# A streaming encoder layer on one core: half the weight differences moved to GpSimd, wider steps at both ends of the state-space loop, gate loads moved to another queue

## The chip, the core and the metric

The kernel runs on one core of a Trainium2 chip. The metric is the device time of one execution in microseconds. TensorE (PE in the rows) multiplies matrices, with a separate row PEld for its weight loads; VectorE (DVE), ScalarE (ACT) and GpSimd (POOL) work element by element; SyncE (SP) mostly issues DMA transfers. Each engine runs its own instructions in order and waits for others by semaphores. PSUM is the memory that PE writes its products to, SBUF the one that tiles live in.

## The reference

One inference step of a one-layer encoder on 2048 new prompt positions and 128 sample positions (8 running streams of 16), with 1024 channels, all in float32:

```
h = RMSNorm(x) * norm_gain
u, g_s, q, k, v, g_a = split(h @ w_in)            # six groups of 512 columns
y_s = S5(u): per channel group a complex diagonal state, h_t = a h_(t-1) + B u_t,
      y = gelu(Re(C h) + D u);  y_s = z_val * sigmoid(z_gate), [z_val, z_gate] = y @ w_glu
y_a = softmax(norm(q) norm(k)^T / 8 + bias(distance)) v      # a band of 9 chunks of 64, 8 heads
y = x + concat[y_s * silu(g_s), y_a * silu(g_a)] @ w_out
```

Outputs are `y`, the newest keys and values, and the final state of the state-space part, for prompt and sample streams.

## The kernel before, in words

The 2176 rows are 17 tiles of 128 (the sample tile first). For accuracy each product of two float32 matrices is three products: every operand is split into a rounded part `hi` and the difference `lo`, and `mm3` (lines 189 to 194) multiplies hi with hi (L192), hi with the weights' lo (L193) and lo with hi (L194).

**The foreground** is a sequence of such products. The input projection runs in three passes over all tiles, with two groups of 512 columns in each: u and k, then v and q, then g_a and g_s. A tile takes 16 calls of `mm3` in a pass, 8 for each group. Then come the GLU (8 calls a tile) and the output projection (16 a tile), 1224 calls in all. After each call `tick` counts a step. Two lists hang on that count: `due` plans the conversions of weight blocks, and `defer` runs a piece of other work some steps later.

**Weights.** A block is 128 rows by 512 columns. `load_w` (L139) loads it by SP's queue into one of five `wraw` buffers, and `conv_w` (L142) makes `whi` on ScalarE and `wlo` on VectorE (L156: raw times gain minus `whi`, in one instruction). The last tile of a pass plans the 16 blocks of the next pass from its step 4 on, 1.25 steps apart, and the background rests until all are issued. Block j of the next pass is numbered from 0 here and is read at step 17 + j of the last tile's count. The load of block j + 5 is issued two steps after the conversion of block j and waits for that buffer.

**Evictions.** Keys and queries are normed: ScalarE squares, VectorE sums (L280), GpSimd takes the power (L281, L282) two steps later, VectorE scales at 8 steps (`zs`, L285), PE transposes at 14 (L295). Keys of the last tiles are also multiplied by a gain on GpSimd (L288) and stored. The gates g_a and g_s are stored to DRAM (L330) from buffers of the tag `plain`.

**The background** is a generator that runs between the steps: the state-space part (`s5`), the decode attention of the 8 sample streams (`decode`), and the band attention. Every foreground step earns credit (650 times a ratio: 0.42 in the state-space loop, 0.75 in decode), and every `yield w` of the background costs w. `SL` is 800 in the state-space part. Its loop has 8 batches of 4 groups, 6 slots a batch. When the u group is done, the loop starts by loading three blocks of u from DRAM (`load_u`, L712), rearranging the first on ScalarE (`perm_u`, L720) and transposing it on PE (`step_a`, L734). In each batch PE makes `v` (L772), VectorE rotates it (L792 to L795), GpSimd makes tables of sine and cosine (L757 to L764). After the loop (L927 to L942) PE transposes the final states (`pf`, `pf2`), VectorE copies them (`of`, `of2`), SP stores them; all three copies use one buffer of the tag `bt`, and all three transposes one PSUM buffer of the tag `ut`. The flag `y`, set at the end, is asked for by the last tile of the third pass, before the first GLU load (L1339).

**The GLU** (`glu`, L1353) loads for each tile the silu gates `gs` (L1376, by SP's queue, into a buffer of the tag `plain`, two of them) when the tile starts, multiplies them into `ms` on GpSimd (L1402) one step into the next tile, and PE transposes `ms` (L1361) after six of the eight steps of that next tile.

Of the kernel before, what the change touches and what calls it, by code (L numbers as in the profile page):

```python
# [7 lines left out]
F32 = mybir.dt.float32  # L8
# [3 lines left out]
OP = mybir.AluOpType  # L12
# [19 lines left out]
def fv(ap):  # L32
    return ap.bitcast(F32)
# [6 lines left out]
class Build:  # L40
# [101 lines left out]
    def conv_w(self):  # L142
        nc = self.nc
        n = self.nconv
        self.nconv += 1
        key, _, k = self.chunks[n]
        raw = self.raws.pop(n)
        hi = self.wp.tile([128, 512], F32R, tag="whi", name="whi", bufs=16)
        lo = self.wp.tile([128, 512], F32R, tag="wlo", name="wlo", bufs=16)
        if k is None:  # L150
            nc.scalar.activation(out=hi, in_=raw, func=AF.Copy)
            nc.vector.tensor_sub(lo, raw, fv(hi))
        else:
            gcol = self.gain[:, k:k + 1]
            nc.scalar.activation(out=hi, in_=raw, func=AF.Copy, scale=gcol)  # L155
            nc.vector.scalar_tensor_tensor(lo, raw, gcol, fv(hi), op0=OP.mult, op1=OP.subtract)  # L156
        self.W[key] = (hi, lo)
        if self.step:
            self.defer(self.T_LW, lambda: self.load_w(n + self.NR))
        elif n + self.NR < 16:  # L160
            self.load_w(n + self.NR)
        else:

            self.defer(40 + 10 * (n + self.NR - 16), lambda: self.load_w(n + self.NR))
# [286 lines left out]
    def s5(self):  # L451
        nc, I, tc = self.nc, self.I, self.tc
# [4 lines left out]
        ps = self.pool(st, "s5ps", side="right", space=PSUM)  # L457
# [91 lines left out]
        g = pp.tile(sh, F32, name="g")  # L549
# [94 lines left out]
        mp = self.pool(st, "s5m", side="right", bufs=2)  # L644
        Tm = []
        for i in range(2):
            t = cp2 = mp.tile([128, GB, 128], F32, name=f"T{i}", bufs=1)
# [3 lines left out]
        CA, VB, VBp, KR, YS = {}, {}, {}, {}, {}  # L651
# [57 lines left out]
        def load_u(b, i):  # L709
            c0, n = BLK[i]  # L710
            u = mp.tile([128, L, GB * CH], F32, tag="U", name="U", bufs=3)
            nc.sync.dma_start(u[0:n], u4[c0:c0 + n, :, b * GB * CH:(b + 1) * GB * CH])  # L712
            U[b, i] = u

        def perm_u(b, i):
            n = BLK[i][1]
            u = U.pop((b, i))
            o = mp.tile([128, GB, L, CH], F32, tag="P", name="P")
            src = u[0:n].rearrange("p j (g h) -> p g j h", g=GB)
            nc.scalar.activation(out=o[0:n], in_=src, func=AF.Copy)  # L720
            P[b, i] = o.rearrange("p g j h -> p g (j h)")
# [131 lines left out]
        SL = self.SL_S5  # L853
# [16 lines left out]
            yield None  # L870
        for n in range(3):
            load_u(0, n)
        yield 2 * SL
        perm_u(0, 0)
        yield SL
        for n in range(3):
            feed(n)
            yield SL
# [48 lines left out]
        pf = ps.tile([32, 128], F32, tag="ut", name="pf")  # L927
        nc.tensor.transpose(pf, FINp, self.ident)
        of = mp.tile([32, 128], F32, tag="bt", name="of", bufs=1)
# [1 line left out]
        nc.sync.dma_start(self.O["rp"], of[:, 0:64])  # L931
        nc.sync.dma_start(self.O["ip"], of[:, 64:128])
        for i in range(2):
            yield 1500
            pf = ps.tile([128, 128], F32, tag="ut", name="pf2")
            nc.tensor.transpose(pf, FINs[:, 4 * i:4 * i + 4].rearrange("p b g -> p (b g)"), self.ident)
            of = mp.tile([128, 128], F32, tag="bt", name="of2", bufs=1)
            nc.vector.tensor_copy(of, pf)
            nc.sync.dma_start(self.O["rs"][128 * i:128 * i + 128], of[:, 0:64])
            nc.sync.dma_start(self.O["is"][128 * i:128 * i + 128], of[:, 64:128])  # L940
# [412 lines left out]
    def glu(self):  # L1353
        nc = self.nc
        W, Z = self.W, {}

        def out(t):
            ms = Z.pop(t)
            pt = self.pst.tile([128, 4, 128], F32, tag="tr", name="tm")
            for k in range(4):  # L1360
                nc.tensor.transpose(pt[:, k], ms[:, 128 * k:128 * k + 128], self.ident)  # L1361
            o = self.ev.tile([128, 8, 128], F32, tag="kt", name="mo", bufs=1)[:, 0:4]
            nc.scalar.activation(out=o.rearrange("p k (c j) -> p k c j", j=L),
                                 in_=pt.rearrange("p k (j c) -> p k c j", j=L), func=AF.Copy, scale=0.5)
            self.defer(2, lambda: nc.sync.dma_start(self.mt_d[t, :, 0:4, :], o))

        for i, t in enumerate(TILES):
            if i == 0:
                self.due(self.step + 16, 10, 8)
            if i == NT - 1:  # L1370
                self.due(self.step + 2, 1.25, 8)
            if i == NT - 2:
                self.out_load(0)
            hi, lo = self.GY.pop(t)
            g = self.ev.tile([128, 512], F32, tag="plain", name="gs")
            nc.sync.dma_start(g, self.gs_d[128 * t:128 * t + 128])  # L1376
            z = {}
            for f in (1, 0):
                z[f] = self.psm.tile([128, 512], F32, tag="mm", name="z")
                for k in range(4):  # L1380
                    self.busy = i == NT - 1
                    self.mm3(z[f], hi[:, k], lo[:, k], W[3, f, k], k == 0, k == 3)
                    self.tick()
                    yield 650
                    if f == 1 and k == 1:
                        if i + 1 < NT:
                            self.glu_conv(TILES[i + 1])
                        else:
                            self.out_conv(0)
                        if i + 2 < NT:  # L1390
                            self.glu_load(TILES[i + 2])
                    if f == 0 and k == 1 and i:
                        out(TILES[i - 1])
                        yield 430
                if f == 1:
                    th = self.ev.tile([128, 512], F32, tag="sq", name="th", bufs=1)
                    nc.scalar.activation(out=th, in_=z[1], func=AF.Tanh, scale=0.5)
            ms = self.ev.tile([128, 1024], F32, tag="vhl", name="ms", bufs=1)[:, 0:512]
            nc.vector.scalar_tensor_tensor(ms, th, 1.0, z[0], op0=OP.add, op1=OP.mult)
            Z[t] = ms  # L1400
            if i + 1 < NT:
                self.defer(1, lambda ms=ms, g=g: nc.gpsimd.tensor_tensor(out=ms, in0=ms, in1=g, op=OP.mult))  # L1402
        nc.vector.tensor_tensor(out=ms, in0=ms, in1=g, op=OP.mult)
        self.defer(4, lambda: out(TILES[-1]))
# [204 lines left out]
```

## Time and profile before

| | us |
|---|---|
| median of 3 runs | 1228.99 (1226.14 to 1230.14) |
| the profiled execution | 1225.45 |
| span of its instructions | 1223.6 |
| mean granted TensorE clock | 0.993 |
| PE, DVE, ACT, POOL busy | 1185.6, 714.5, 610.6, 364.2 |

The order of the work in the trace, in us from the span's start: first pass to about 207, second to about 456, third to 702, GLU to 873, output projection to the end. The state-space loop runs from about 218 to 590, decode from 608 to 670, attention from 715 to 1166. A row's bracket gives how long the engine idled before it and who released it. `PEclk` is the clock that TensorE was granted, as a share of full speed.

### The profile page before, as it was taken

To read this page: it belongs to the slowest core of one execution; us is meant where nothing else is said; L and a number is where in the kernel's file an instruction comes from. 1 tells how busy PE (TensorE), PEld (TensorE's weight loads), DVE (VectorE), ACT (ScalarE), POOL (GpSimd) and SP (SyncE) were. 2 spreads that over 40 slices of the span, in tenths; PEclk is the share of its full clock that TensorE was granted. 3 is DMA by queue.
4 is the path that set the end of the run, shared out by engine and by line. 5 is a ranking of instruction groups with operands and counts; after the bars stand their busy time and mean duration, and the time that the engine had idled before them with its cause. 6 is when DMAs were issued, how large, how long until landed. Compare 5 with 4: busy or idle time off the path is not lost.

```text
span 1223.6 us, 18141 instructions
## 1 busy us (share of the span) xinstructions
PE 1185.6 (97%) x6363; PEld 973.3 (80%) x6363; DVE 714.5 (58%) x1358; ACT 610.6 (50%) x1177; POOL 364.2 (30%) x407
## 2 busy tenths in 40 slices
PE   8999999899999999999899999999999999999998
PEld 6888888678788887787667878788788788888887
DVE  5476627489888888963234336665655555555511
ACT  6435436465555666553243446555655455555510
POOL 2433562267757647530000011111211111111120
PEclk9999999999999999999999999999999999999999
DMA  7765456757466778445796598998578687778143
GB/s 251 241 193 167 150 169 202 219 140 168 119 170 159 160 223 196 103 111 94 212 349 232 160 270 247 265 263 228 196 227 237 185 221 231 211 210 256 57 132 117
DMA packets 250018, 236.78 MB, mean 194 GB/s; under 512 B 111256, under 2 KB 184736, under 8 KB 248904
## 3 DMA queue, kind: packets, MB, share of 16 engines
q1 hardware_dynamic: 248408, 232.16, 66.4%
q0 software_dynamic: 1376, 3.47, 1.0%
q8 instruction: 50, 0.82, 0.3%
q14 instruction: 40, 0.33, 0.1%
q10 hardware_dynamic: 144, 0.00, 0.0%
HBM read 169.48 MB, written 68.06 MB: 194 GB/s over the span
## 4 chain that ended last, share of the span: by engine, by line
PE 78%; DMA 9%; DVE 5%; ACT 4%; SPq 3%; issue 2%; POOL 0%; DVEq 0%; ACTq 0%; POOLq 0%
PE z L192 18%; PE z L194 18%; PE z L193 18%; PE o L1221 5%; PE pt L1203 5%; PE s L1173 5%; DMA wraw<-in_w_in_dram 3%; PE pt L295 1%; PE v L772 1%; PE y L841 1%; PE y L840 1%; DMA mt<-mt_d 1%; PE o L1062 1%; DMA vc<-in_vc_dram 1%; DVE hlo L232 1%
## 5 line engine op out<-in xcount | busy, mean ns | idle before, releaser
L192 PE MATMUL z<-whi,hhi 128*128 128x512 f32 x816 | 342.0, 419 | 0.8 <-ACT whi L155 0.7
L193 PE MATMUL z<-wlo,hhi 128*128 128x512 f32 x816 | 321.1, 394 | 2.4 <-DVE wlo L156 2.4
L194 PE MATMUL z<-whi,hlo 128*128 128x512 f32 x816 | 320.9, 393 | 0.0
L192 PEld LDWEIGHTS z<-whi,hhi 128*128 128x128 f32 x816 | 154.5, 189 | 36.3 <-issue 3.3
L193 PEld LDWEIGHTS z<-wlo,hhi 128*128 128x128 f32 x816 | 154.5, 189 | 35.6 <-DVE wlo L156 6.1
L194 PEld LDWEIGHTS z<-whi,hlo 128*128 128x128 f32 x816 | 154.1, 189 | 33.7
L1210 ACT ACTIVATE pth<-pt 128x640 fp32r<-128x640 f32 (+4 forms) x128 | 81.7, 638 | 133.8 <-PE pt L1203 95.5
L1211 DVE TENSOR_TENSOR ptl<-pt,pth 128x640 fp32r<-128x640 f32 (+4 forms) x128 | 94.5, 739 | 54.2 <-ACT pth L1210 53.2
L1192 ACT ACTIVATE sn<-sn,mn 128x640 f32<-128x640 f32 (+4 forms) x128 | 96.9, 757 | 36.0 <-DVE mn L1183 34.1
L192 PE MATMUL z<-whi,mh 128*128 128x512 f32 x272 | 114.4, 420 | 0.0
L194 PE MATMUL z<-whi,ml 128*128 128x512 f32 x272 | 107.5, 395 | 0.0
L193 PE MATMUL z<-wlo,mh 128*128 128x512 f32 x272 | 107.2, 394 | 0.0
L1183 DVE CUSTOM_DVE_ANT_0 sn<-s,bias 128x640 f32<-128x640 f32 (+4 forms) x128 | 93.2, 728 | 7.2 <-PE s L1173 7.0
L1203 PE MATMUL pt<-ident,sn 128*128 128x128 f32 x560 | 83.1, 274 | 9.7 <-DVE ptl L1211 6.4
L1402 POOL TENSOR_TENSOR ms<-ms,gs 128x512 f32<-128x512 f32 x16 | 20.7, 1291 | 230.9 <-DMA gs<-gs_d 119.5
L1173 PE MATMUL s<-ks,q 128*128 128x320 f32 (+1 forms) x448 | 88.1, 313 | 0.2 <-DVE mn L1183 0.2
L1203 PEld LDWEIGHTS pt<-ident,sn 128*128 128x128 f32 x560 | 64.7, 140 | 29.5 <-ACT sn L1192 12.8
L1173 PEld LDWEIGHTS s<-ks,q 128*128 128x128 f32 x448 | 75.5, 189 | 13.1 <-DVE mn L1183 3.0
L1417 POOL TENSOR_TENSOR ml<-mt,mh 128x1024 fp32r<-128x1024 f32 x17 | 40.6, 2390 | 126.8 <-ACT mh L1416 95.1
L232 DVE TENSOR_TENSOR hlo<-xraw,hhi 128x1024 fp32r<-128x1024 f32 x49 | 60.8, 1241 | 20.7 <-ACT hhi L229 18.8
L1238 POOL TENSOR_TENSOR ga<-ga,sum 128x512 f32<-128x512 f32 x16 | 16.7, 1044 | 171.6 <-DVE sum L1236 123.6
L281 POOL TENSOR_SCALAR s<-s 128x8 f32<-128x8 f32 x34 | 15.1, 445 | 176.5 <-DVE s L280 176.1
(261 smaller groups left out, 2111.7 us busy)
## 6 DMA issues: line engine op xcount, KB each, us to landing
xraw<-in_xT_dram SPq DMA_DIRECT2D x49, 512.0 KB
q<-qt_d SPq DMA_DIRECT2D x64, 256.0 KB
ks<-kt_d SPq DMA_DIRECT2D x28, 512.0 KB
vhl<-vp_d SPq DMA_DIRECT2D x28, 512.0 KB
wraw<-in_w_in_dram SPq DMA_DIRECT2D x48, 256.0 KB
bias<-tl_d SPq DMA_DIRECT2D x32, 320.0 KB
mt<-mt_d SPq DMA_DIRECT2D x17, 512.0 KB
x<-in_x_dram SPq DMA_DIRECT2D x34, 256.0 KB
```

Source lines behind the costliest of these rows:

```text
L192: mm(z, a, whi, start=first, stop=False)
L193: mm(z, a, wlo, start=False, stop=False)
L194: mm(z, b, whi, start=False, stop=last)
L232: nc.vector.tensor_sub(lo, raw, fv(hi))
L1173: nc.tensor.matmul(ps_s[:, bank, 0:wp], Q[n, x2][:, s, 128 * a:128 * a + 128], KS[n][:, s, c0:c0 + wp], start=(x2 == 0), stop=(x2 == 1))
L1183: nc.vector.tensor_tensor_reduce(out=o, in0=i0, in1=i1, scale=1.0, scalar=3e38, op0=OP.add, op1=OP.min, accum_out=mn)
L1192: nc.scalar.activation(out=sn[:, 0:w], in_=sn[:, 0:w], func=AF.Exp, scale=-1.0, bias=mn, accum_out=SUM[n][:, a, s:s + 1])
L1203: nc.tensor.transpose(t[:, k], pr[:, 128 * k:128 * k + 128], self.ident)
L1210: nc.scalar.activation(out=h, in_=t[:, 0:w], func=AF.Copy)
L1211: post.append(lambda: nc.vector.tensor_tensor(out=l, in0=t[:, 0:w], in1=fv(h), op=OP.subtract))
L1221: nc.tensor.matmul(o[:, a0:a1], VB[n][:, j, s, :], t[:, 3 * a0 + j + a0:4 * (a1 - 1) + j + 1:4], start=(y == 0 and j == 4), stop=(y == 1 a ...
L1417: self.defer(2, lambda: self.nc.gpsimd.tensor_tensor(out=lo, in0=m, in1=fv(hi), op=OP.subtract))
```

## The change

At input pass changes (the first index of the block's key is 1 or 2) the `lo` of odd blocks is made on GpSimd in two instructions, the first of which overwrites `raw`. At the start of the state-space loop 5 SL instead of 2 SL lie between the loads of u and the first `perm_u`, and 2 SL instead of one behind it. At its end 2500 instead of 1500 of credit lie ahead of each of the last two transposes, these use PSUM buffers of the tags `y` and `v` (two each), and the first of the two copies uses a buffer of the tag `VB` (two of them). The load of the GLU's gates is issued by GpSimd's queue.

```diff
@@ conv_w @@
-            nc.vector.scalar_tensor_tensor(lo, raw, gcol, fv(hi), op0=OP.mult, op1=OP.subtract)
+            if key[0] and n % 2:
+
+                nc.gpsimd.tensor_scalar(raw, raw, gcol, None, op0=OP.mult)
+                nc.gpsimd.tensor_tensor(out=lo, in0=raw, in1=fv(hi), op=OP.subtract)
+            else:
+                nc.vector.scalar_tensor_tensor(lo, raw, gcol, fv(hi), op0=OP.mult, op1=OP.subtract)
@@ s5, start of the loop @@
         for n in range(3):
             load_u(0, n)
+        yield 5 * SL
+        perm_u(0, 0)
         yield 2 * SL
-        perm_u(0, 0)
-        yield SL
         for n in range(3):
             feed(n)
             yield SL
@@ s5, end @@
         for i in range(2):
-            yield 1500
-            pf = ps.tile([128, 128], F32, tag="ut", name="pf2")
+            yield 2500
+            pf = ps.tile([128, 128], F32, tag=("y", "v")[i], name="pf2", bufs=2)
             nc.tensor.transpose(pf, FINs[:, 4 * i:4 * i + 4].rearrange("p b g -> p (b g)"), self.ident)
-            of = mp.tile([128, 128], F32, tag="bt", name="of2", bufs=1)
+            of = mp.tile([128, 128], F32, tag=("VB", "bt")[i], name="of2", bufs=(2, 1)[i])
@@ glu @@
             g = self.ev.tile([128, 512], F32, tag="plain", name="gs")
-            nc.sync.dma_start(g, self.gs_d[128 * t:128 * t + 128])
+            nc.gpsimd.dma_start(g, self.gs_d[128 * t:128 * t + 128])
```

## Rows read from the trace of the kernel before

**Rows 1.** The page's part 1: busy us, share of the span, instructions.
```profile
PE 1185.6 (97%) x6363; PEld 973.3 (80%) x6363; DVE 714.5 (58%) x1358; ACT 610.6 (50%) x1177; POOL 364.2 (30%) x407
```

**Rows 2.** Timeline of PE at four places: start, duration, instruction, [idle before <- releaser].
```profile
216.62 0.50 PE L193 MATMUL z<-wlo,hhi 128*128 128x512 f32 x1 [0.46 <-DVE wlo L156]
...
219.27 0.63 PE L295 MATMUL pt<-ident,zs 128*128 128x128 f32 x4 [1.93 <-DVE zs L285]
...
224.57 1.11 PE L734 MATMUL ut<-ident,P 128*128 128x128 f32 x4 [3.29 <-ACT P L720]
...
465.71 0.72 PE L772 MATMUL v<-UT,VB 128*128 128x272 f32 x2 [2.32 <-DVE t L792]
...
585.78 0.33 PE L936 MATMUL pf<-ident,FINs 128*128 128x128 f32 x1 [2.32 <-DVE of L938]
...
714.80 0.65 PE L1361 MATMUL tm<-ident,ms 128*128 128x128 f32 x4 [2.50 <-POOL ms L1402]
```

**Rows 3.** Windows: length; busy (count) of PE, PEld, DVE, ACT, POOL; clock, DMA, GB/s.
```profile
224.38:227.79 3.41, 3.22 (x10) 2.74 (x11) 1.54 (x4) 3.38 (x7) 0.09 (x1) 0.50 1.05 349
...
715.90:719.31 3.41, 3.16 (x9) 1.95 (x8) 1.24 (x2) 2.12 (x4) 0.00 (x0) 0.50 1.05 353
978.73:982.14 3.41, 3.41 (x12) 2.81 (x11) 1.99 (x4) 1.68 (x4) 0.66 (x1) 0.50 1.06 187
```

**Rows 4.** Single lines over the whole span: count, duration in ns minimum/median/maximum.
```profile
L156 DVE SCALAR_TENSOR_TENSOR wlo<-wraw,gain,whi x48: 741/751/1876, 4.9 to 463.5; 128x512 fp32r<-128x512 f32 x48
...
L1402 POOL TENSOR_TENSOR ms<-ms,gs x16: 1256/1296/1305, 713.5 to 868.0; 128x512 f32<-128x512 f32 x16
...
L281 POOL TENSOR_SCALAR s<-s x34: 192/197/1399, 33.1 to 460.0; 128x8 f32<-128x8 f32 x34
...
L282 POOL TENSOR_TENSOR s<-s,nhalf x34: 1636/1678/2732, 34.2 to 460.7; 128x8 f32<-128x8 f32 x34
...
L762 POOL TENSOR_TENSOR sin<-sb,cb x32: 609/798/1602, 147.3 to 526.8; 128x256 f32<-128x256 f32 x32
```

**Rows 5.** Timelines of ACT, DVE and POOL at the first pass change.
```profile
197.86 2.56 ACT L155 ACTIVATE whi<-wraw,gain 128x512 fp32r<-128x512 f32 x4
...
202.58 2.54 DVE L156 SCALAR_TENSOR_TENSOR wlo<-wraw,gain,whi 128x512 fp32r<-128x512 f32 x2
202.62 1.29 POOL L288 TENSOR_TENSOR plain<-zs,kgrow 128x512 f32<-128x512 f32 x1 [3.40 <-ACT whi L155]
...
223.88 0.63 ACT L720 ACTIVATE P<-U 128x512 f32<-128x512 f32 x1 [6.14 <-DMA U<-u_d]
```

**Rows 6.** Timelines of POOL and PE at the second pass change.
```profile
444.50 2.05 POOL L282 TENSOR_TENSOR s<-s,nhalf 128x8 f32<-128x8 f32 x1
...
450.21 0.60 PE L295 MATMUL pt<-ident,zs 128*128 128x128 f32 x4
457.48 0.62 PE L772 MATMUL v<-UT,VB 128*128 128x272 f32 x2
...
467.14 1.05 PE L295 MATMUL pt<-ident,zs 128*128 128x128 f32 x4
```

**Rows 7.** DVE's timeline at the loop's end; line L1339 over the whole span.
```profile
585.43 0.29 DVE L938 COPY of<-pf 128x128 f32<-128x128 f32 x1 [8.86 <-DMA out_dram<-of]
...
L1339 SPq DMA_DIRECT2D y<-y_d x17: 370/431/599, 689.7 to 841.3; - x17
```

**Rows 8.** Chain and SP's timeline at the GLU's start; DMA issues (KB each, us to landing).
```profile
704.69 8.65 DMA gs<-gs_d
...
714.77 0.34 SPq L1376 DMA_DIRECT2D gs<-gs_d  x1
...
tl_d<-rl_d POOLq DMA_DIRECT2D x8, 383.5 KB, 5.4
...
rl_d<-rl POOLq DMA_DIRECT2D x1, 24.0 KB, 2.8
```

## The prediction

> **What bounds the kernel now.** I read the page's engine totals first: TensorE (PE) is busy 1185.6 of 1223.6 us and no other engine over 60% [rows 1], so the time is that of PE's stream, and only time in which PE waits or runs slowly can be won: 38.0 us of waits, plus what the clock takes. The timeline of PE then says where the long waits lie. The reader is to see three places in [rows 2] where one wait is 2.3 us or more beside a cause that the diff touches (585.8, 714.8 and 465.7), and a fourth, around 216 to 225, where three waits follow each other (0.46, 1.93 and 3.29). Third, the windows on the granted clock: after each of these four places, and once more at 978.73, there are 3.41 us at a granted clock of 0.50, the lower of the two levels (1.2 of 2.4 GHz) [rows 3] (three of the five stand there); PE had idled 2.32, 2.50 or 3.29 us just before, while after the wait of 1.93 us it went on at the upper level. 3.41 us at half speed lose 1.71 us each.
>
> So the four places cost: first pass change 0.46 + 1.93 + 3.29 + 1.71 = 7.4; second pass change 2.32 + 1.71 = 4.0; end of the state-space loop 2.32 + 1.71 = 4.0; start of the GLU 2.50 + 1.71 = 4.2. Together 19.6 us. The sum is made against the profiled execution, 1225.45 us with a span of 1223.6; the median of the runs shown is 3.54 us above it, and I carry the difference over to that median.
>
> A scheduling step is three products. From the turn's transposes at 450.21 (after step 14 of a tile, 0.45 us in all) to the first background product at 457.48 (after step 24) there are ten: (7.27 - 0.45) / 10 = 0.68 us of PE each [rows 6]. In the state-space phase it gives the background 0.42 x 650 = 273 of credit.
>
> **Wider step at the loop's start.** At 224.57 PE waits for `ut`, which waits for `perm_u` on ScalarE, which sat 6.14 us until the first U block landed [rows 5]. The transposes are issued 3 SL = 2400 of credit after the loads, 8.8 steps; in the change 7 SL = 5600, 20.5 steps, so 11.7 steps or 8.0 us of products more lie between. That is over the 6.14 us waited, so this wait (3.29) goes. The cost of the later start is put at nothing: the loop's end gates the foreground only at the first GLU load, issued at 689.7 [rows 7], while the loop's last transposes stand at 585.8 [rows 2]; 19 steps (below) are 13 us of over 100.
>
> **Half the differences on GpSimd (POOL).** Eight of sixteen at each change leave VectorE, 8 x 0.751 = 6.0 us per change [rows 4], and become two POOL instructions each. The second is like L1402 (same shape, two inputs): 1.296. The first, one input over 512 columns, is not in the trace; the bounds are 0.197 (8 columns, L281) and 1.296 (two inputs, L1402); I take half of the latter, 0.65, as it reads half as much. What VectorE does meanwhile stretches POOL: L762 takes 0.609 alone and 0.798 at the median. I add 0.25 to each of the two (0.19 for 256 columns, rounded up for 512): 2.44 us per block. Bounds: 0.197 + 1.296 = 1.5, and 2 x 1.296 + 1.0 (both stretched by L762's maximum less its minimum, 0.99, in half of them) = 3.6.
>
> These blocks stand in POOL's queue with the power of the key or query norm (L281 and L282, 0.197 + 1.678, up to 2.7 beside VectorE [rows 4]; I take 2.2 for both), which is issued between blocks 11 and 13. Queued behind it are block 13, block 15 and the sine tables; VectorE's `zs` waits for the power, PE for `wlo`. PE reads block j at step 17 + j of the last tile's count; the turn's transposes (L295) follow step 30, so the product just ahead of them reads block 13.
>
> First change: PE reads `wlo` 13 at 216.62, already 0.46 late [rows 2]. POOL can start block 1 when the first ScalarE conversions are done, at about 199.2 [rows 5]; six blocks are 14.6, the key product in between 1.29, so block 11 ends near 215.1, the power (2.2) 217.3, block 13 219.7, block 15 222.2. Before, block 15 was read some 1.4 us after the transposes of 219.27, at 220.7. PE thus reaches it 1.5 later (1.7 with the clock), the 1.93 lies inside the new wait, the 3.29 and its clock fall go, and a wait of some 3.5 us brings a clock fall of its own, already paid in the 1.7 but for 0.3: 1.7 + 0.3 - 3.3 - 1.7 = -3.0. From the bounds: at 1.5 per block nothing waits but `zs` behind the power, -6.5; at 3.6 block 15 ends at 231.5, +10.8 - 5.0 = +5.8.
>
> Second change: POOL is free of the last power at 446.55 [rows 6]; block 11 ends at 461.2, the power 463.4, block 13 465.8, block 15 468.3. The wait of 2.32 for VectorE's `t` goes, since the last difference and `zs` no longer stand ahead of it so long; PE comes to block 13 about 462.5 (457.48, five steps of 0.68, and some 1.6 us of background products between) and waits to 465.8. Before, it read it about 466.5 (the step ahead of the turn at 467.14) and block 15 about 469.5 (two steps at the lower clock later). So the place breaks even: 0. Bounds: -4.0 at 1.5 per block; at 3.6, block 15 at 477.6, +8.
>
> The raw buffers of odd blocks come free about 1.7 us later, and SP's in-order queue holds the next loads with them; costed at nothing because the load of the last block hangs on blocks 5 and 10, of which one is odd (inside the bounds otherwise).
>
> VectorE and POOL share something: L156 takes 0.741 at best and 1.876 at most [rows 4]; the two of it at 202.58 take 2.54 where POOL's key product of 1.29 runs beside them [rows 5]. The Trainium skill, "SBUF — State Buffer", section "Who interferes with whom", says that a VectorE instruction with two SBUF inputs and a GpSimd instruction that reads SBUF shut each other out for a whole instruction. By that rule the two engines' times add, 1.94 + 0.75 for a pair of blocks and what else VectorE takes between, towards the 3.2 per block of the late-POOL rival below, 1229. The trace agrees for that one pair of rows; L762's median, 0.798 against a maximum of 1.602, says that most do not wait that long.
>
> **Wider step and other buffers at the loop's end.** At 585.78 PE waits 2.32 for VectorE's copy `of2`, which had waited 8.86 for the store of the one `bt` buffer [rows 2, 7]. The first `of2` now takes a VB buffer that nothing uses, the second `bt` 5000 / 273 = 18.3 steps = 12.5 us after `of`, more than the 8.86 us that the release took. PE's transposes get PSUM buffers of their own. -4.0. If SP's queue ran 3.6 us later the wait would come back in part: bounds -4.0 to 0.
>
> **Gates by POOL's queue.** PE waits at 714.80 for `ms`, POOL's product, which waited for the gate load of 704.69, 8.65 us on its way [rows 2, 8]. On POOL's queue it is issued no later. The landing of a load of 256 KB there isn't shown; bounds are 2.8 us (24 KB, the shortest of that queue) and 8.65 (as now), the nearest is 5.4 us for 383.5 KB [rows 8]: landed at 710.1, product done at 711.4, PE comes at 712.1. -4.2; if not, 0. New order on POOL: the next tile's load is issued ahead of the product. It waits for a buffer: in tile 1 that is held by the last silu store; behind it waits the first product, and PE for that. POOL, busy 30% [rows 1], has room for the 17 issues. SP loses 17 issues and a hold: at 714.77 it waited for that product with a bias load behind it [rows 8]. Attention's first loads, 19 steps later now, no longer crowd these.
>
> The Trainium skill, "DMA: Bandwidth & Descriptors", section "Issuing engines are not separate DMA queues", says that DMAs from all engines interleave on the same sixteen, and that another issuer saves its issue time only. By that the load lands as late as now and this part gives 0; no run here shows 256 KB on both queues.
>
> **The rest.** 4 SL = 11.7 steps and 2000 / 273 = 7.3 more shift the loop, the decode stage and attention against the tiles. PE's other waits are 38.0 - 12.8 = 25 us over 1224, about 2 per 100 us; some 490 us are re-drawn, 10 us of waits. I take +1 (bounds -3 and +4).
>
> **Sum:** -3.0 + 0 - 4.0 - 4.2 + 1 = -10.2, so 1215.3 for the profiled execution and **1219** for the median. Its own range: 1214 to 1225.
>
> **Rivals.**
> *POOL is cheap* (1.5 to 1.7 per block): -6.5 - 4.0 - 4.0 - 4.2 + 1 = -17.7, 1211. For it: POOL is idle 70%. Against: the power in its queue, and L762's stretch.
> *The gates land no earlier* (the transfers share engines, or the first load is held for the store): -6.0, 1223. For it: the chain shows this load as slow, not its issue as late. Against: the transfers crowding it move away.
> *POOL becomes the late one at both changes*, slower: the price is eight times what a block takes over 2.44, in each change. At 3.2 per block +2.6 and +5, with -8.2 + 1: no change; from there on slower, at 3.6 5.8 + 8 - 8.2 + 1 = +6.6, 1236. For it: L156's 1.876; the rule of the Trainium skill on the shared port ("SBUF — State Buffer") leads here. Against: VectorE has eight such instructions fewer to bring at each change.
> *Re-phasing eats it*: the loop's VectorE-heavy part falls just behind the second change: +5 instead of +1, and 0 from the start of the GLU: -2, 1227.
>
> **Chances.** Forecast 0.50 (faster 0.46, same 0.04); cheap POOL 0.17 (faster); late gates 0.13 (0.09, 0.04); late POOL 0.15 (same 0.06, slower 0.09); re-phasing 0.05 (0.02, 0.02, 0.01). A measurement of this kernel tells 0.3%, 3.7 us, from no change: faster 0.74, same 0.16, slower 0.10. Range 1210 to 1230: the cheap case inside its lower end, late POOL up to no change inside its upper end.
>
> **What would show it.** Right: no PE wait for `ut`, `pf` or the first `tm`; three stretches at 0.50 instead of five; waits for `wlo` of some 3 us just ahead of the turn's transposes at both changes, on POOL. Wrong: POOL blocks of 1.7 us with no wait for `wlo` (too little forecast), or of over 3 us; the gate load landing after 8 us; waits for `t` or `zs` behind the second change.

## The result: slower by 0.9%

The changed kernel takes 1238.56 us (1237.42 to 1239.15), the kernel before, run beside it, 1227.57: ratio 1.0091, interval 1.0075 to 1.0106. 1219 with a range of 1210 to 1230 was forecast.

### The profile page after: what moved, and what is told of

It is laid out like the page before. It is cut to its first block, busy times and chain, and to the rows that moved or that the text cites. A ratio compares the mean times of both kernels' runs of the same rounds, so it can differ in the third digit from the quotient of the medians.

```text
span 1236.2 us, 18182 instructions
## 1 busy us (share of the span) xinstructions
PE 1189.3 (96%) x6363; PEld 974.1 (79%) x6363; DVE 712.5 (58%) x1342; ACT 611.9 (50%) x1177; POOL 426.8 (35%) x456
## 4 chain that ended last, share of the span: by engine, by line
PE 85%; DMA 4%; ACT 3%; DVE 3%; POOL 2%; issue 2%; SPq 0%; POOLq 0%; DVEq 0%; ACTq 0%
PE z L197 21%; PE z L199 20%; PE z L198 20%; PE o L1226 5%; PE pt L1208 5%; PE s L1178 5%; DMA wraw<-in_w_in_dram 2%; POOL wraw L158 1%; PE pt L300 1%; PE y L845 1%; PE y L846 1%; PE v L777 1%; PE o L1067 1%; DMA mt_d<-mo 1%; PE ut L739 1%
## 5 line engine op out<-in xcount | busy, mean ns | idle before, releaser
L197 PE MATMUL z<-whi,hhi 128*128 128x512 f32 x816 | 342.2, 419 | 0.2
L198 PE MATMUL z<-wlo,hhi 128*128 128x512 f32 x816 | 322.4, 395 | 19.4 <-POOL wlo L159 17.6
L199 PE MATMUL z<-whi,hlo 128*128 128x512 f32 x816 | 321.2, 394 | 0.0
L197 PEld LDWEIGHTS z<-whi,hhi 128*128 128x128 f32 x816 | 154.2, 189 | 35.5 <-issue 3.3
L199 PEld LDWEIGHTS z<-whi,hlo 128*128 128x128 f32 x816 | 154.2, 189 | 33.6 <-DVE hlo L237 0.3
L197 PE MATMUL z<-whi,mh 128*128 128x512 f32 x272 | 115.3, 424 | 1.9 <-ACT mh L1421 1.9
L199 PE MATMUL z<-whi,ml 128*128 128x512 f32 x272 | 107.9, 397 | 1.9 <-POOL ml L1422 1.9
L286 POOL TENSOR_SCALAR s<-s 128x8 f32<-128x8 f32 x34 | 11.3, 332 | 157.2 <-DVE s L285 156.7
L1236 DVE TENSOR_TENSOR ot<-o,tmp 64x512 f32<-64x512 f32 x32 | 22.0, 689 | 74.7 <-ACT tmp L1234 74.7
```

What stands on the lines that cost most here:

```text
L197: mm(z, a, whi, start=first, stop=False)
L198: mm(z, a, wlo, start=False, stop=False)
L199: mm(z, b, whi, start=False, stop=last)
```

## The profile after

The changed kernel's lines stand five below those of before from L162 on: the differences are L158 and L159 on POOL and L161 on VectorE, `mm3` is L197 to L199. PE's timeline at the two pass changes, the answer to the first rows of [rows 2]:

```profile
214.00 0.51 PE L198 MATMUL z<-wlo,hhi 128*128 128x512 f32 x1 [1.67 <-POOL wlo L159]
...
216.89 0.50 PE L198 MATMUL z<-wlo,hhi 128*128 128x512 f32 x1 [1.24 <-POOL wlo L159]
...
220.78 0.50 PE L198 MATMUL z<-wlo,hhi 128*128 128x512 f32 x1 [2.21 <-POOL wlo L159]
...
226.25 0.79 PE L198 MATMUL z<-wlo,hhi 128*128 128x512 f32 x1 [2.98 <-POOL wlo L159]
...
470.91 0.50 PE L198 MATMUL z<-wlo,hhi 128*128 128x512 f32 x1 [1.27 <-POOL wlo L159]
...
477.33 0.80 PE L198 MATMUL z<-wlo,hhi 128*128 128x512 f32 x1 [4.32 <-POOL wlo L159]
```

None of the waits of [rows 2] is left at its place. In their place PE waits for odd blocks made by POOL, ten times, 17.6 us together. The windows of the changed kernel, the two pass changes, the stretch from the loop's end through decode, and the end of attention (columns as in [rows 3]):

```profile
205.00:240.00 35.00, 26.81 (x105) 20.17 (x104) 12.73 (x17) 14.32 (x22) 26.52 (x19) 0.85 0.73 223
440.00:490.00 50.00, 40.54 (x172) 31.32 (x171) 32.02 (x47) 27.72 (x51) 39.81 (x31) 0.97 0.70 202
560.00:700.00 140.00, 140.00 (x1050) 108.44 (x1049) 53.44 (x138) 54.75 (x100) 0.96 (x1) 1.00 0.68 211
1160.00:1200.00 40.00, 34.25 (x161) 27.29 (x160) 10.63 (x19) 8.09 (x13) 5.79 (x3) 0.96 0.29 96
```

The last two of the same windows in the kernel before:

```profile
560.00:700.00 140.00, 134.58 (x1019) 103.57 (x1018) 42.32 (x109) 48.77 (x83) 0.96 (x1) 0.99 0.70 218
1160.00:1200.00 40.00, 38.83 (x179) 31.85 (x180) 8.13 (x14) 6.07 (x8) 9.50 (x5) 1.00 0.42 135
```

From the loop's end through decode PE never stops now (140.00 of 140.00, before 134.58); at attention's end it works 34.25 of 40 us, before 38.83. The lower clock at the first change lasts far longer than the 3.41 us of [rows 3]:

```profile
221.30:231.45 10.15, 7.17 (x19) 5.21 (x19) 2.65 (x4) 1.89 (x3) 8.87 (x6) 0.50 0.68 205
```

To add up such places I take, for each microsecond of the profile, what PE idled plus its busy time x (1 - granted clock), and call it lost:

| place (us) | before | changed | difference | forecast |
|---|---|---|---|---|
| first pass change, 205 to 240 | 7.2 | 11.8 | +4.6 | -3.0 |
| second pass change, 440 to 490 | 4.3 | 11.1 | +6.7 | 0 |
| loop's end and decode, 490 to 700 | 7.8 | 0.0 | -7.8 | -4.0 |
| start of the GLU, 700 to 750 | 4.5 | 6.0 | +1.4 | -4.2 |
| end of attention, 1160 to 1200 | 1.2 | 7.4 | +6.2 | in the +1 |
| all else | 20.6 | 20.4 | -0.2 | in the +1 |
| sum | 45.6 | 56.7 | +11.0 | -10.2 |

The profiled spans differ by 12.6; 1.6 us of it are not in this table. A place repeats to about 2 us, little more than a clock fall, from one execution to the next: four kernels below that change nothing ahead of 560 us lose 6.8 to 9.1 and 2.6 to 4.8 at the two pass changes, where the kernel before loses 7.2 and 4.3.

At the start of the GLU the wait for the first gated product is gone, but attention's first score now waits for VectorE, and PE goes on at the lower clock (0.50 from 737.37 to 741.00):

```profile
737.37 0.79 PE L1178 MATMUL s<-ks,q 128*128 128x256 f32 x2 [2.85 <-DVE mn L1188]
```

POOL's timeline shows the cause at the first change:

```profile
212.68 1.26 POOL L159 TENSOR_TENSOR wlo<-wraw,whi 128x512 fp32r<-128x512 f32 x1
213.92 1.57 POOL L158 TENSOR_SCALAR wraw<-wraw,gain 128x512 f32<-128x512 f32 x1
215.58 1.26 POOL L159 TENSOR_TENSOR wlo<-wraw,whi 128x512 fp32r<-128x512 f32 x1
216.82 1.57 POOL L158 TENSOR_SCALAR wraw<-wraw,gain 128x512 f32<-128x512 f32 x1
218.47 2.26 POOL L159 TENSOR_TENSOR wlo<-wraw,whi 128x512 fp32r<-128x512 f32 x1
220.81 0.20 POOL L286 TENSOR_SCALAR s<-s 128x8 f32<-128x8 f32 x1
221.09 1.68 POOL L287 TENSOR_TENSOR s<-s,nhalf 128x8 f32<-128x8 f32 x1
222.76 2.08 POOL L158 TENSOR_SCALAR wraw<-wraw,gain 128x512 f32<-128x512 f32 x1
224.93 1.26 POOL L159 TENSOR_TENSOR wlo<-wraw,whi 128x512 fp32r<-128x512 f32 x1
```

In these rows a block is 2.9 to 3.9 us, not the 2.44 forecast, and PE's waits above end where the subtractions end. Behind the sixth stands the power (L286, L287), behind that block 13, for which PE waits longest (2.98). The two lines over the whole span (columns as in [rows 4]):

```profile
L158 POOL TENSOR_SCALAR wraw<-wraw,gain x16: 1566/2004/2650, 199.2 to 477.3; 128x512 f32<-128x512 f32 x16
...
L159 POOL TENSOR_TENSOR wlo<-wraw,whi x16: 1262/1285/2256, 201.3 to 480.0; 128x512 fp32r<-128x512 f32 x16
```

Together 53.5 us in 16 blocks, 3.34 each. The instruction that I took at 0.65 takes 1.57 at best and 2.00 at the median.

## Experiments

Medians in us of 6 or 12 executions; the kernel before was run beside each group of four, and the ratio is to that.

| kernel | median | before | ratio, interval |
|---|---|---|---|
| no_pool | 1223.2 | 1226.4 | 0.9966, 0.9944 to 0.9987 |
| pool_only | 1239.6 | 1226.4 | 1.0097, 1.0073 to 1.0121 |
| steps_only | 1221.6 | 1226.4 | 0.9956, 0.9934 to 0.9979 |
| gates_only | 1229.9 | 1226.4 | 1.0020, 0.9999 to 1.0042 |
| start_only | 1233.9 | 1226.2 | 1.0064, 1.0045 to 1.0084 |
| end_only | 1218.3 | 1226.2 | 0.9931, 0.9907 to 0.9955 |
| pool_quarter | 1230.7 | 1226.2 | 1.0036, 1.0022 to 1.0049 |
| pool_bcast | 1230.3 | 1226.2 | 1.0041, 1.0026 to 1.0057 |
| pool_to11 | 1230.9 | 1225.9 | 1.0044, 1.0022 to 1.0066 |
| end_start4 | 1220.6 | 1225.9 | 0.9950, 0.9928 to 0.9971 |
| end_start3 | 1227.4 | 1225.9 | 1.0008, 0.9987 to 1.0029 |
| all_margin | 1227.9 | 1225.9 | 1.0020, 1.0004 to 1.0036 |
| end_margin | 1214.8 | 1225.9 | 0.9911, 0.9889 to 0.9933 |
| end_pool3 | 1223.4 | 1225.9 | 0.9978, 0.9963 to 0.9994 |
| end_gates | 1220.2 | 1225.9 | 0.9957, 0.9936 to 0.9977 |

### Each part alone

**no_pool**: the change without its first hunk.

```diff
-            if key[0] and n % 2:
...
-            else:
-                nc.vector.scalar_tensor_tensor(lo, raw, gcol, fv(hi), op0=OP.mult, op1=OP.subtract)
+            nc.vector.scalar_tensor_tensor(lo, raw, gcol, fv(hi), op0=OP.mult, op1=OP.subtract)
```

> All of the change but the differences on GpSimd. Price theory (GpSimd's 3.3 us per odd block paces both pass changes, where TensorE loses 11.8 and 11.1 us by waits and clock): the first change falls back to the two early waits of before, 2.4 us, the second to about 4.3, so 16.2 us less than the changed kernel: 1222 us, and no wait for wlo over 0.5. Re-phasing theory (the later background, not GpSimd's price, is what made it slower): it stays above the kernel before, 1230 us or more, with the waits near the end of attention (5.8 us of idle from 1160 to 1200) still there.

**pool_only**: the kernel before with that hunk alone.

```diff
+            if key[0] and n % 2:
+                nc.gpsimd.tensor_scalar(raw, raw, gcol, None, op0=OP.mult)
+                nc.gpsimd.tensor_tensor(out=lo, in0=raw, in1=fv(hi), op=OP.subtract)
...
```

> The kernel before with the differences of odd blocks at the pass changes on GpSimd and nothing else. Price theory: +4.6 at the first change (the wait for the first U block lies inside the new waits) and +6.7 at the second: 1239 us, as slow as the whole change, with the waits of 2.3 at the loop's end and 2.5 at the first GLU product still there. Re-phasing theory: half of that at most, 1233 or less.

In their totals both came out as the price theory has it: without POOL's blocks 1223.2, with nothing but them 1239.6. The GpSimd part costs 12 to 15 us (by ratios and by medians), as much as the whole loss or more. The end of attention still loses 5.5 in no_pool, so that part of the re-phasing theory held as well.

By places the theory fits less well. It put no_pool at 2.4 and 4.3 at the pass changes, and no_pool loses 3.9 and 8.1; pool_only loses 14.7 and 9.2 there, and 4.1 more than the kernel before from 490 to 700. So in the changed kernel POOL's blocks add 7.9 at the first change and 3.0 at the second. The other 3.8 at the second (8.1 against 4.3) come with the step at the loop's start: steps_only loses 8.0 there, start_only 6.8. In these kernels SP issues transfers for the loop (U and T, nine of them from 436.84 to 443.36 in no_pool) shortly ahead of the weight loads, and ScalarE waits longer for block 5. Its timelines, in the kernel before and in no_pool:

```profile
450.55 2.80 ACT L155 ACTIVATE whi<-wraw,gain 128x512 fp32r<-128x512 f32 x4 [2.88 <-DMA wraw<-in_w_in_dram]
```

```profile
451.64 2.82 ACT L155 ACTIVATE whi<-wraw,gain 128x512 fp32r<-128x512 f32 x4 [6.93 <-DMA wraw<-in_w_in_dram]
```

The same wait is 6.51 in steps_only, 5.17 in start_only and 5.35 in the changed kernel, where POOL too starts block 5 after a wait of 2.54 for its load (457.85). That this order in SP's queue makes up the 3.8 is read from the traces and wasn't tested.

**steps_only** and **gates_only**: the kernel before with the two hunks of the state-space loop, and with the last hunk.

```diff
-        yield 2 * SL
+        yield 5 * SL
         perm_u(0, 0)
-        yield SL
+        yield 2 * SL
...
-            yield 1500
+            yield 2500
```

> The kernel before with both wider steps of the state-space part and nothing else. By the ledger of the changed kernel: -5.0 (wait for ut and its clock fall) -4.0 (loop's end) and, if the later attention costs what it shows there, +1.4 at its first scores and +6.2 at its end: 1226 us. If the waits at attention's start and end come from the GpSimd part or the gates instead: 1218.5.

```diff
-            nc.sync.dma_start(g, self.gs_d[128 * t:128 * t + 128])
+            nc.gpsimd.dma_start(g, self.gs_d[128 * t:128 * t + 128])
```

> The kernel before with the gate loads on GpSimd's queue and nothing else. If the queue brings them early enough: the wait of 2.5 us for the first gated product goes with its clock fall, 1223.4 us. If the transfers share what they shared before: within 1 us of the kernel before, 1227.6, with that wait still over 1.5 us.

steps_only lies between its two numbers; in its trace PE no longer waits for the first gated product, though SP still loads the gates: the first load goes out at 694.38, ahead of attention's first `q` loads at 705.52. So the steps, not the queue, took that wait away. gates_only made it longer. POOL's timeline there, and PE's product behind it:

```profile
698.40 0.59 POOL L1376 DMA_DIRECT2D gs<-gs_d  x1 [103.70 <-DMA gs_d<-plain]
716.97 0.55 POOL L1376 DMA_DIRECT2D gs<-gs_d  x1 [17.98 <-DMA gs_d<-plain]
717.54 1.27 POOL L1402 TENSOR_TENSOR ms<-ms,gs 128x512 f32<-128x512 f32 x1
```

```profile
718.87 1.12 PE L1361 MATMUL tm<-ident,ms 128*128 128x128 f32 x4 [5.55 <-POOL ms L1402]
```

The first load goes out 6.3 us earlier than in [rows 8], but the second then holds POOL's queue for 17.98 us, until its buffer is stored, and the first product, queued behind it, cannot start before 717.54. PE waits 5.55 where it waited 2.50.

**start_only** and **end_only** part the two steps.

> The kernel before with the wider step at the loop's start alone. Both theories: the wait for ut and its clock fall go (-5). Price theory of the pair of steps: the 12 steps of shift are what makes the wait for zs at the second change 3.3 us instead of the 2.3 for t (+3.7 with the clock), and the loop's end keeps its 4.0: 1225. If the shift at the second change comes from the other step: 1221.

> The kernel before with the wider step, the PSUM and the SBUF buffers at the loop's end alone. The wait of 2.3 for of2 and its clock fall go (-4.0) and everything ahead of 560 us stays as it was, so 1222.4; if 7 steps of delay are enough to move the attention loads off the first gate load, that wait goes too: 1218. If the end of attention then waits as it does with both steps (+2.2): 1220 to 1225.

The edits are the first and the second half of the hunks above. end_only gains more than the wait and its clock fall: what is lost from 560 to 700 falls from 7.1 to 1.7, and the wait for the first gated product goes too. start_only is slower than the kernel before, and outside both of its numbers. The wait for `ut` goes, as forecast, but PE's timeline shows what comes instead, the first of these with 2.8 us more lost to the clock:

```profile
597.41 0.48 PE L936 MATMUL pf<-ident,FINs 128*128 128x128 f32 x1 [5.08 <-DVE of L938]
...
729.28 0.80 PE L1173 MATMUL s<-ks,q 128*128 128x256 f32 x2 [3.65 <-DVE mn L1183]
```

The second is attention's first score, and 1160 to 1200 loses 6.7. Of the 7.7 us by which the profiled span is longer, the end of attention makes +5.5, the second change +2.5, the start of the GLU +1.9 and the first change -2.7; from 490 to 700 the kernel loses 7.8, as before. The wait of 5.08 is for the one `bt` buffer. SP issues the store that frees it 9.4 us after the copy (594.39 after 585.03), behind eight stores of y begun at 584.78; before, it was 5.4 us (581.98 after 576.57).

### What a block on POOL costs

**ts_imm**, **pool_bcast**: the first of the two instructions in two other forms; ts_imm leaves the gain out of these differences.

```diff
-                nc.gpsimd.tensor_scalar(raw, raw, gcol, None, op0=OP.mult)
+                nc.gpsimd.tensor_scalar(raw, raw, 1.0, None, op0=OP.mult)
```

> The whole change with the constant 1 in place of the gain column in GpSimd's first instruction (the gain is left out of these differences). If reading the column is what makes it 1.57 us alone and 2.0 beside VectorE: 1.3 or less, and no longer where VectorE is busy at its start. If it is the one-input form itself: 1.5 to 1.6 again, still 2.0 where it starts during a VectorE instruction.

```diff
-                nc.gpsimd.tensor_scalar(raw, raw, gcol, None, op0=OP.mult)
+                nc.gpsimd.tensor_tensor(out=raw, in0=raw, in1=gcol.to_broadcast([128, 512]), op=OP.mult)
```

> The whole change, but the product with the gain is made by an instruction with two tensor inputs (the gain column repeated along the row) instead of one with a column scalar. If that form takes the 1.27 us of the subtraction, a block costs 2.6 instead of 3.3, and each change is shorter by up to 8 x 0.75 = 6 us: 1227 to 1231. If two instructions with two inputs shut VectorE out, or are shut out, for as long: a block still costs 3.2 or more, 1236 or more.

The lines over the span, of ts_imm with one row of POOL's timeline behind it, then of pool_bcast:

```profile
L158 POOL TENSOR_SCALAR wraw<-wraw x16: 1487/1499/2038, 199.4 to 474.2; 128x512 f32<-128x512 f32 x16
...
210.17 1.94 POOL L158 TENSOR_SCALAR wraw<-wraw 128x512 f32<-128x512 f32 x1
```

```profile
L158 POOL TENSOR_TENSOR wraw<-wraw,gain x16: 1030/1318/1526, 200.2 to 471.8; 128x512 f32<-128x512 f32 x16
...
L159 POOL TENSOR_TENSOR wlo<-wraw,whi x16: 1261/1600/1753, 201.8 to 473.3; 128x512 fp32r<-128x512 f32 x16
```

With a constant the one-input form still takes 1.49 at best, so it is the form that is slow; the column adds 0.08. The stretch beside VectorE stays: the seven of the 16 that started 0.06 us or more into a two-input VectorE instruction took 1.93 to 2.04 (the row above started at 210.17, VectorE's difference ran from 209.50 to 210.76), the other nine 1.49 or 1.50. The median falls from 2.00 to 1.50 because fewer started so. That is ts_imm's second theory. With two inputs the product takes 1.03 alone, but then the subtraction's median rises from 1.29 to 1.60. ts_imm, in one run, took 1232.35; pool_bcast is 6 to 8 us below the whole change (by ratios and by medians), as its first theory had the time; a block takes 2.78 on average, between the 2.6 and the 3.2 of the two theories.

**pool_quarter**, **pool_to11**: fewer blocks on POOL, in the whole change.

```diff
-            if key[0] and n % 2:
+            if key[0] and n % 4 == 1:
```

> The whole change with only blocks 1, 5, 9 and 13 on GpSimd, the other twelve on VectorE. Queue theory (GpSimd is late only because 8 blocks of 3.3 us do not fit ahead of PE's reads): 4 blocks take 13.4 us, the first three are done ahead of PE's first read of them, so no wait for wlo over 1 us: 1223, as without the GpSimd part. Linear theory (each block moved costs its share): half of the loss stays, 1231.

```diff
-            if key[0] and n % 2:
+            if key[0] and n % 2 and n % 16 < 12:
```

> The whole change, but blocks 13 and 15, the two that stand behind the power of the key or query norm in GpSimd's queue, stay on VectorE. Place theory (what stands behind the power costs most): the waits of 2.98 and 4.32 us and the lower clock behind them go, those for the blocks up to 11 stay (5.1 and 4.7 us): 10 us less than the whole change, 1228. Share theory (six of eight blocks cost six eighths of the 16 us): 1234.5.

pool_quarter's time is what the linear theory says, but its rows are those of a queue: PE's long waits are both for block 13, the one behind the power:

```profile
224.11 0.79 PE L198 MATMUL z<-wlo,hhi 128*128 128x512 f32 x1 [4.67 <-POOL wlo L159]
...
472.84 0.80 PE L198 MATMUL z<-wlo,hhi 128*128 128x512 f32 x1 [5.18 <-POOL wlo L159]
```

pool_to11 takes that block away, and at the first change 6.8 us are lost instead of 11.8, as the place theory has it; the time lies between the two theories. At the second change nothing is won (12.6 against 11.1): six of VectorE's instructions for the state-space loop, 471.33 to 477.99, are late next, and PE waits for what follows them (DVE's timeline, then PE's):

```profile
471.33 1.17 DVE L664 TENSOR_TENSOR CA<-PB,ArS 128x576 f32<-128x576 f32 x1
...
477.00 0.99 DVE L675 TENSOR_TENSOR VBp<-VBp,btmp 128x512 f32<-128x512 f32 x1
```

```profile
478.38 1.27 PE L777 MATMUL v<-UT,VB 128*128 128x272 f32 x2 [3.84 <-DVE t L797]
```

**end_pool3**: the loop's end with only blocks 1, 5 and 9 on POOL, all ahead of the power.

```diff
+            if key[0] and n % 16 in (1, 5, 9):
+                nc.gpsimd.tensor_scalar(raw, raw, gcol, None, op0=OP.mult)
+                nc.gpsimd.tensor_tensor(out=lo, in0=raw, in1=fv(hi), op=OP.subtract)
...
```

> The loop's end alone, with the differences of blocks 1, 5 and 9 of each pass change on GpSimd, all ahead of the power in its queue. If three blocks at 3.3 us fit (place theory): no wait for wlo on GpSimd, and as VectorE's last difference waits for its load there, nothing is gained: 1218 +- 2. If VectorE's eight instructions were what kept zs and t late: 1213. If GpSimd beside VectorE stretches both: 1222 or more.

PE waits for POOL only 0.7 us now, and still the kernel is slower than end_only (0.9978 against 0.9931, the intervals apart). Two of VectorE's differences take 2.31 us where the subtraction of a POOL block runs beside them and 1.41 where none does, and PE waits 3.12 for `t`, further back in VectorE's queue, and goes on at the lower clock:

```profile
460.79 2.31 DVE L160 SCALAR_TENSOR_TENSOR wlo<-wraw,gain,whi 128x512 fp32r<-128x512 f32 x2 [1.81 <-ACT whi L155]
...
465.41 1.41 DVE L160 SCALAR_TENSOR_TENSOR wlo<-wraw,gain,whi 128x512 fp32r<-128x512 f32 x2
```

```profile
469.57 1.27 PE L776 MATMUL v<-UT,VB 128*128 128x272 f32 x2 [3.12 <-DVE t L796]
```

The second change loses 5.7 us here and 2.6 in end_only. How much of that is the stretch isn't shown: VectorE's last difference there also waits for its load, and kernels with neither POOL's blocks nor the start's step lose up to 4.8 at this place. The two profiled executions differ by 1.5 us only (1221.93 and 1220.40), so they hold little of the 5 us between the medians.

### The phase of the background

**end_start4**, **end_start3**: the loop's end with a smaller step at its start.

```diff
-        yield 2 * SL
+        yield 4 * SL
```

> The kernel before with the loop's end of the change, and at its start 4 SL and one SL in place of 5 and 2: a shift of 5.9 steps, not 11.7. 2 SL more are 4.0 us, more than the 2.3 that is waited there for ut. If only the shift by 12 steps brought the wait of 3.2 for zs at the second change: ut's wait and its clock fall go from the 1218.3 of the loop's end alone, 1214. If any shift brings such a wait: 1218 or more.

> The same with 3 SL and one SL: 2.9 steps, 2.0 us. Ut's wait falls to about 0.3 with no clock fall, and the shift is a quarter of the change's: 1214.5; 1218 or more if any shift brings a wait at the second change.

end_start3 has 3 SL there. Neither beats end_only: the wait for `ut` goes in end_start4 and falls to 0.36 in end_start3, and others come, behind it (236.34) or at the second change (PE's timelines of end_start3 and end_start4):

```profile
236.34 0.72 PE L772 MATMUL v<-UT,VB 128*128 128x272 f32 x2 [3.33 <-ACT UT L735]
```

```profile
462.34 1.27 PE L772 MATMUL v<-UT,VB 128*128 128x272 f32 x2 [4.39 <-DVE t L792]
```

**all_margin**, **end_margin**: attention's credit aims at an end eight steps earlier.

```diff
-    MARGIN = 0
+    MARGIN = 8
```

> The whole change with attention told to be done 72 steps before the end instead of 64 (MARGIN 8 for 0). Slot theory (the 6 us lost from 1160 to 1200 come from the load of the output projection's next tile, which is asked for at two fixed steps of eight and just missed the first of them after attention's last store): attention is done 8 steps, 5.4 us, earlier, the load goes out in time, the waits of 1.9 and 1.7 and their clock fall go: 1232.5. If the load is slow for another reason (queue, landing): the waits stay, 1238.

> The loop's end alone, with the same MARGIN 8. Slot theory: 6.4 us lost from 1160 to 1200 fall to about 1.2: 1213. Otherwise 1218.

In the changed kernel the output projection's next tile is waited for after attention's end; PE's timeline, and SP's:

```profile
1184.71 0.50 PE L197 MATMUL z<-whi,mh 128*128 128x512 f32 x1 [1.90 <-ACT mh L1421]
...
1187.14 0.69 PE L199 MATMUL z<-whi,ml 128*128 128x512 f32 x1 [1.70 <-POOL ml L1422]
```

```profile
1169.89 5.60 SPq L1256 DMA_DIRECT2D mt_d<-mo  x3
1178.13 0.35 SPq L1478 DMA_DIRECT2D out_dram<-o  x1
1178.53 0.42 SPq L1461 DMA_DIRECT2D x<-in_x_dram  x1
1179.06 0.40 SPq L1414 DMA_DIRECT2D mt<-mt_d  x1
```

The load of that tile (L1414) goes out 9.2 us after SP began attention's last stores, behind a store and a load of the projection itself. In the kernel before, with the same 76 steps left after attention's last transposes, it goes out 6.2 us after them, about one slot of four steps (4 x 0.68) sooner:

```profile
1162.90 5.61 SPq L1251 DMA_DIRECT2D mt_d<-mo  x3
1169.09 0.33 SPq L1409 DMA_DIRECT2D mt<-mt_d  x1
```

With eight steps more the lost time there is gone in both; the window of all_margin and of end_margin:

```profile
1160.00:1200.00 40.00, 38.65 (x179) 31.83 (x180) 8.31 (x14) 5.18 (x7) 8.22 (x4) 1.00 0.44 146
```

```profile
1160.00:1200.00 40.00, 40.00 (x178) 33.11 (x177) 4.84 (x7) 4.25 (x4) 9.57 (x4) 1.00 0.46 154
```

end_margin is the fastest kernel found. It is 2 to 4 us below end_only (by ratios and by medians), less than the 6.4 that end_only loses there, and the intervals of the two overlap; all_margin is 9 to 11 below the whole change, of which 6.1 are this place; the rest isn't explained.

In all_margin the load goes out 8.5 us after SP began attention's last stores (1171.62 after 1163.08), still behind a store and a load of the projection. What the margin gives is room. After attention's last transposes 83 steps are left (five tiles of 16 and 3), not 76 (four and 12), so by steps of 0.68 us the load goes out some 13 steps ahead of the tile that needs it, not 6 (an estimate). That a load one slot sooner is enough by itself is seen in the kernel before only.

**end_gates**: the loop's end with the gates on POOL's queue (the edit of gates_only).

> The loop's end alone, with the gate loads on GpSimd's queue. The first gated product no longer waits once the end is moved (1.1 us lost in all from 700 to 750), so the queue has nothing to give: 1218. If the second gate load, held for its buffer at the head of GpSimd's queue, keeps the first product as in the gates alone (wait of 5.6 us): 1222 or more.

2 to 3 us over end_only, and the intervals overlap: nothing gained, and a loss that these runs don't settle. Its trace has the wait of the second theory, though a smaller one: POOL issues the second gate load at 706.81, the first product starts behind it at 707.38, and PE waits 2.42 for that (708.71); end_only's PE doesn't wait there.

## Why the prediction was wrong

**The price of a POOL block** is the step that failed: "I take half of the latter, 0.65, as it reads half as much", with 1.296 as the upper bound. It measured 1.57 at best, so the bound was wrong too: that an instruction reads less is no reason that it takes less. The mechanism was on record as the late-POOL rival, and its own rule (eight times what a block takes over 2.44, in each change) gives with 3.34 -3.0 + 7.2 = +4.2 and 0 + 7.2 = +7.2; +4.6 and +6.7 were measured. The sum is right; that each half fits is partly luck, since POOL's blocks add 7.9 and 3.0 over no_pool, and the start's step makes up the second. With its other terms as forecast the rule gives 4.2 + 7.2 - 8.2 + 1 = +4.2, 1233; the rest up to +11.0 is the gates (5.6) and the end of attention (some 5), less 3.8 gained at the loop's end. The rival's figures for 3.2, +2.6 and +5, are not what its rule gives: that is +3.1 and +6.1, 2 us slower and not no change. That rival had a chance of 0.15, and its end at 3.6 (1236) was cut off by the range, at 1230.

**The place in the queue** was right: block 13 waits behind the power, and that wait is the longest at both changes. Block 15 costs PE little (0.43 us in the second change, at 481.42). That earlier blocks would be late as well followed only from the higher price.

**VectorE's side.** "VectorE has eight such instructions fewer to bring" was counted as relief. end_pool3 shows none. In the changed kernel two VectorE differences, the first started 0.43 us after a POOL subtraction (the row of POOL ahead of it), the second 0.54 us after a POOL product with the column:

```profile
209.33 1.29 POOL L159 TENSOR_TENSOR wlo<-wraw,whi 128x512 fp32r<-128x512 f32 x1
...
209.76 1.40 DVE L161 SCALAR_TENSOR_TENSOR wlo<-wraw,gain,whi 128x512 fp32r<-128x512 f32 x1 [1.96 <-ACT whi L155]
...
214.46 0.75 DVE L161 SCALAR_TENSOR_TENSOR wlo<-wraw,gain,whi 128x512 fp32r<-128x512 f32 x1 [2.63 <-ACT whi L155]
```

The first is nearly doubled, the second is not. The Trainium skill, "SBUF — State Buffer", section "Who interferes with whom", lets any POOL instruction that reads SBUF shut out a VectorE instruction with two inputs. The first row agrees (it ends 0.54 us after POOL's, at 211.16), the second doesn't: POOL's product from 213.92 to 215.49 held nobody up. Four more differences that started inside a product of 1.57 us took 0.75 to 0.77.

**The loop's end** was right in its wait and its clock fall (-4.0) and too small in all: decode behind it lost 3 us more that went as well.

**The loop's start** removed its wait as forecast. "The cost of the later start is put at nothing" failed: it looked only at what gates the foreground next, not at where VectorE's work, attention's first scores and attention's last store fall, 12 steps later, nor at what SP's in-order queue then holds ahead of the weight loads and of `bt`'s store. Alone this step makes the kernel 0.64% slower.

**The gates**: -4.2 was booked to POOL's queue. The prediction named the second load ahead of the first product and priced it at nothing; alone it costs 3 us of wait. The wait went in the whole change because the steps moved attention's loads behind the gates'. The 6.0 lost there are attention's first score: 2.85 of wait and some 3 by the clock.

**Re-phasing** was taken at +1, -3 to +4, as a share of small waits. The end of attention alone is +6.2; the rows lay that to one load that missed a slot.

Not settled: whether the start's step would pay with the loop's transfers behind the weight loads at the second change, or which of VectorE's instructions would have to move there. Moving the power out of POOL's queue wasn't tried.

## What to carry to other kernels

An operation that the trace doesn't show on an engine has no upper bound from rows of other operations there: measure it alone before half of a burst is moved to that engine, and look at what stands in its in-order queue between the moved pieces. Test the parts of a change one at a time: here one part gave -0.7%, one +1.0%, and the sum hid both. A shift of a background by some steps is not free because nothing waits for its end; look for the places where it hands over by slots, and at what its loads and stores then stand ahead of in the queue that issues them.

## What was not expected of the hardware

- On POOL 512 columns with one tensor input and a column scalar take 1.57 us, with a constant 1.49, the subtraction with two tensor inputs 1.26, and the product with a repeated column 1.03.
- The one-input instruction took 1.57 each of the six times that VectorE was idle at its start, and 2.0 to 2.65 the ten times that VectorE was in a two-input instruction at its start or began one within 0.04 us.
- After the third of three waits (1.67, 1.24 and 2.21, at 214.00, 216.89 and 220.78) the granted clock fell to the lower level, and stayed there for 10.15 us, with 2.98 us of idle inside; in the kernel before a wait of 1.93 at 219.27, with one of 0.46 at 216.62, was followed by no fall.
